# One first transfer for weight half, tokens and gains; conv pieces ahead of the query's; latent transposes five steps behind the key's

## The chip, the cores and the metric

The kernel runs on one core of a Trainium2 chip. The metric is the device time of one execution in microseconds (us): the median of several runs, and beside it the time of the one execution that was profiled. The profile calls the engines PE (TensorE, matmuls), DVE (VectorE), ACT (ScalarE), POOL (GpSimd) and SP (SyncE, which here only issues DMA transfers).

## The reference

Two layers of a streaming-encoder trunk over 256 tokens of width 1024, all in float32. In each layer one combined projection feeds four mixers (latent attention a, pooling b, a spatial gating unit c, a short convolution d), and four gates; then a SwiGLU network follows.

```python
def reference(x, w_in, g_pre_mix, g_cq, g_ckv, w_uq, w_ukv, ...):
    for l in range(DEPTH):
        h = rmsnorm(x, g_pre_mix[l])
        (c_q, c_kv, k_r, p_in, s_u, s_v, cv_b, cv_c, cv_x,
         gate_logits) = split_cols(h @ w_in[l])
        y_a = mla_branch(c_q, c_kv, k_r, g_cq[l], g_ckv[l], w_uq[l], w_ukv[l], cos, sin) @ w_br_a[l]
        y_b = pool_branch(p_in, pool_w[l], pool_scale[l]) @ w_br_b[l]
        y_c = sgu_branch(s_u, s_v, g_sgu_v[l], sgu_w[l], sgu_b[l]) @ w_br_c[l]
        y_d = conv_branch(cv_b, cv_c, cv_x, conv_w[l]) @ w_br_d[l]
        gates = jax.nn.sigmoid(gate_logits).reshape(B, S, N_BRANCH, D)
        merged = (gates[:, :, 0] * y_a + gates[:, :, 1] * y_b
                  + gates[:, :, 2] * y_c + gates[:, :, 3] * y_d)
        x = x + rmsnorm(merged @ w_out[l], g_post_mix[l])
        h = rmsnorm(x, g_pre_ffn[l])
        f = (jax.nn.silu(h @ w_ffn_gate[l]) * (h @ w_ffn_up[l])) @ w_ffn_down[l]
        x = x + rmsnorm(f, g_post_ffn[l])
    return x
```

In mla_branch the latents c_q (256 wide) and c_kv (128) are normalised before the products with w_uq and w_ukv, and the 32 columns of k_r become the rotary part of the key.

## The kernel before, in words

**Weights.** All weights come through in 268 pieces of 128 partitions and up to 1024 columns, in the order of a list (PLAN, from piece_plan). A piece is named by its group: A (latents and rotary key), S (gating unit), P and C (pool and convolution inputs), uq and ukv (the latent attention's second products), g (gates), y (branch products), and so on to the feed-forward. SP issues its transfer into one of four buffers "st"; ACT copies it to a rounded high half (convert, L268), and DVE subtracts this from the piece for the low half (settle, L288). Both halves lie in buffers of the pool "u4", 24 of them. The tokens are split into high and low halves in the same way ("hh" and "hl"), and a product is three matmuls: high by high, low by high, high by low (mac, L318 to L320).

**Order.** One Python program writes the instructions of all engines in order; each engine then runs its own in that order and waits for the others by semaphores. The main line writes matmul units: a unit is one piece for one half of the tokens (h = 0 or 1, 128 tokens each) and mostly six matmuls. After each unit, tick() lets background generators go on by a step, and calls for the next conversions when few converted pieces are ahead. `yield n` in a generator means "go on after n more ticks". Two generators matter here. g_proj belongs to the attention: it normalises the latents (L658 and L659), transposes the rotary keys, copies them into the key's buffers (L665), waits PA ticks, transposes the latents of half 0 and of half 1 (three blocks each, one tick between) and splits them with a gain (split_scaled: ACT L447, DVE L448), then does the query products. g_misc belongs to the other mixers: it transposes z (the convolution's product, two blocks) and p (four blocks) of each half, with copies by ACT at L790, L795 and L796. Both write transposes (L440) through one pool "tp" of two PSUM buffers. The eight PSUM banks are four accumulators "acc", two "mm" and these two.

**Start.** Seven matmuls on zeros warm TensorE up (L387). ACT's queue loads the first 128 rows of the transposed tokens and a table "cst" of 158 columns (rotary tables and all gains); SP's queue loads the first two weight pieces in halves, with the other tokens between. DVE scales the first token block by its gain out of cst (x_hi, L561), ACT converts the first weight halves (L581), and the first matmuls (L909) start.

Of the kernel before, what the change touches and what calls it, by code (L numbers as in the profile page):

```python
# [31 lines left out]
PIECE = 1024  # L32
POOL_W = (2, 4, 8, 16)
PAD = 16
NST = 4
# [3 lines left out]
GF = 5  # L39
GY, MY, AY, AS, MS = 4, 4, 4, 8, 3  # L40
Y1, Y2, Y3, Y4, Y5 = 2, 4, 3, 3, 3
PA, PB = 2, 4
SA, SB = 3, 3
NW = 7
EV = 2
XAT, XD = (8, 9), 8
RN = 1
# [18 lines left out]
SG = {}  # L66
# [4 lines left out]
SGW = _o  # L71


def down_after(b):

    return [b - DLAG] if 0 <= b - DLAG < NB - DLAST else []


def piece_plan():

    plan = []
    for l in range(NL):
        wd = {g: 2 * sum(b - a for a, b in cols) for g, cols in GROUPS}
        if l == 0:
            plan += [((l, g, i), wd[g]) for i in range(4) for g in "AS"]
        else:
            plan += [((l, g, i), wd[g]) for g in "AS" for i in range(4)]
        plan += [((l, "P", i), wd["P"]) for i in range(4)]
        plan += [((l, "uq", i), 1024) for i in range(2)]
        plan += [((l, "ukv", 0), 1024)]  # L90
        plan += [((l, "C", i), wd["C"]) for i in range(4)]
        lag = []
        for br in BRS:
            for n in range(2):
                plan += [((l, "g" + br, n, i), 1024) for i in range(4)] + lag
                lag = [((l, "y" + br, n, i), 1024) for i in range(2 if br == "a" else 1)]
        plan += lag
        for kp in range(2):
# [95 lines left out]


@with_exitstack
def trunk(ctx: ExitStack, tc, x, xT, wall, small, const, qtab, gpost, out):
    nc = tc.nc
    PS = bass.MemoryType.PSUM
    cp = ctx.enter_context(tc.tile_pool(name="cp", bufs=1))  # L200
# [156 lines left out]


    ident = T([P, P], "ident", 1, pool=cp)
    cst = T([P, 96 + NL * SGW], "cst", 1, pool=cp)  # L360
    warm = T([P, 1], "warm", 1, pool=cp)
    ht = [hT_tiles(h) for h in range(2)]
    state["free"] -= 2
# [2 lines left out]
    def xt_load(eng, k0, k1):  # L366
        eng.dma_start(xt[k0 // 4][:, k0 % 4:k0 % 4 + k1 - k0, :], xT[:, k0:k1, :])

    xt_load(nc.scalar, 0, 1)
    nc.scalar.dma_start(cst, const)  # L370
    stage_part(0, 0)
    stage_part(1, 0)
    xt_load(nc.sync, 1, 2)
    stage_part(0, 1)
    stage_part(1, 1)
    state["dma"] = 2
    xt_load(nc.sync, 2, 4)
    stage_to(4)
    xt_load(nc.sync, 4, 6)
    xt_load(nc.sync, 6, 8)  # L380
    wt = tok()
    nc.vector.memset(wt[:, 0:P], 0.0)
    nc.vector.memset(warm, 0.0)
# [170 lines left out]
    sg = gains(0)  # L554
    hT, rstd = [None, None], [None, None]

    def x_hi(k, eng=nc.scalar):
        for h in range(2):
            o, i, g = ht[h][0][:, k, :], xt[k // 4][:, k % 4, h * P:(h + 1) * P], sg["gpm"][:, k:k + 1]
            if eng is nc.vector:  # L560
                nc.vector.tensor_scalar(o, i, g, None, op0=ALU.mult)  # L561
            else:
                nc.scalar.activation(o, i, AF.Identity, scale=g)

    def x_lo(k):
        for h in range(2):
            nc.vector.scalar_tensor_tensor(ht[h][1][:, k, :], xt[k // 4][:, k % 4, h * P:(h + 1) * P],
                                           sg["gpm"][:, k:k + 1], ht[h][0][:, k, :].bitcast(F32),
                                           op0=ALU.mult, op1=ALU.subtract)


    first_w = {i: (U([P, PIECE], F32R), U([P, PIECE], F32R)) for i in range(2)}
    state["free"] -= 4
    src = [staged.pop(i) for i in range(2)]
    for k in range(2):
        x_hi(k, nc.vector if k == 0 else nc.scalar)
        x_lo(k)
        for i in range(2):
            w = PLAN[i][1] // 2
            c = np.s_[:, k * w:k * w + w]  # L580
            nc.scalar.activation(first_w[i][0][c], src[i][c], AF.Copy)  # L581
            nc.vector.tensor_tensor(first_w[i][1][c], src[i][c], first_w[i][0].bitcast(F32)[c], op=ALU.subtract)
    for i in range(2):
        known(i, *first_w[i])
    state["cv"] = 2
    stage_to(5)
    for kp in range(1, 4):
        for k in range(2 * kp, 2 * kp + 2):
            x_hi(k)
            x_lo(k)  # L590
        pump(2)
        settle()
# [601 lines left out]
def build(arrays):  # L1194
    import concourse.bacc as bacc

    nc = bacc.Bacc("TRN2", target_bir_lowering=False, num_devices=1)
    ap = {k: nc.dram_tensor(k, v.shape, F32, kind="ExternalInput").ap() for k, v in arrays.items()}
    out = nc.dram_tensor("out", (SEQ, D), F32, kind="ExternalOutput").ap()
    with tile.TileContext(nc) as tc:  # L1200
        trunk(tc, ap["x"], ap["xT"], ap["wall"], ap["small"], ap["const"], ap["qtab"], ap["gpost"], out)
    return nc


def host_arrays(inputs):
    inp = {k: np.asarray(v) for k, v in inputs.items()}
    wall = np.zeros((len(PLAN), P, PIECE), np.float32)
    for i, (key, w) in enumerate(PLAN):
        wall[i, :, :w] = host_piece(inp, key)
    x = np.ascontiguousarray(inp["x"][0])  # L1210
    const, qtab = host_const(inp)
    return {
        "x": x,
        "xT": np.ascontiguousarray(x.T.reshape(NK, P, SEQ).transpose(1, 0, 2)),
        "wall": wall,
        "small": np.stack([host_small(inp, l) for l in range(NL)]),
        "const": const,
        "qtab": qtab,
        "gpost": np.ascontiguousarray(np.stack([inp["g_post_mix"], inp["g_post_ffn"]], axis=1)),
    }  # L1220
# [9 lines left out]
```

## Time and profile before

| | us |
|---|---|
| median of 3 runs | 802.88 (802.56 to 804.34) |
| the profiled execution | 802.21 |
| its span in the profile | 800.4 |
| mean granted TensorE clock | 0.998 |
| ACT busy, mean of one L268 conversion | 452.6, 1.047 |
| DVE busy, mean of one L288 | 598.3, 1.214 |

The span runs from the first to the last recorded instruction; the rest of the execution's time, 1.81 us, lies around it. Busy times are sums over the span. [...]

### The profile page before, as it was taken

The numbers are of one execution on the slowest core, as the hardware profiler recorded it, in microseconds if no ns is written. First come the engines' busy times: TensorE is split into PE (matmuls) and PEld (weight loads), VectorE is DVE, ScalarE is ACT, GpSimd is POOL, SyncE is SP. The second block draws the span as 40 slices with busy tenths as digits, with TensorE's granted clock in tenths as the row PEclk, the third lists the DMA queues.
The fourth block names the chain that finished last, engine by engine and source line by source line (L and its number), as shares of the span: only waits on it lengthen the run. The fifth ranks groups of instructions, "written<-read, shape, count | busy, mean of one in ns | idle before, by whom it ended". The sixth has DMA issues, their size and how long they took to land.

```text
span 800.4 us, 10903 instructions
## 1 busy us (share of the span) xinstructions
PE 790.8 (99%) x3982; PEld 666.3 (83%) x3982; DVE 598.3 (75%) x1094; ACT 452.6 (57%) x776; POOL 3.9 (0%) x16
## 2 busy tenths in 40 slices
PE   8999999999999999999999999999999999999996
PEld 8888887888888888888888888878888888888885
DVE  6687976758887777778895688764679787777773
ACT  7767655444665555455665675644367555455541
POOL 0000000000000000000000000000000000000000
PEclk9999999999999999999999999999999999999999
DMA  9866444465664565555655545455555555555631
GB/s 317 304 215 212 160 158 158 160 208 164 201 214 136 185 205 185 186 192 176 223 170 197 205 161 182 131 172 197 175 193 184 181 185 186 187 185 185 206 106 52
DMA packets 42245, 148.11 MB, mean 185 GB/s; under 512 B 4688, under 2 KB 5840, under 8 KB 42192
## 3 DMA queue, kind: packets, MB, share of 16 engines
q1 hardware_dynamic: 41328, 145.12, 54.4%
q0 software_dynamic: 576, 2.10, 0.8%
q8 instruction: 31, 0.51, 0.3%
q10 hardware_dynamic: 288, 0.21, 0.1%
q14 instruction: 22, 0.18, 0.1%
HBM read 146.36 MB, written 1.05 MB: 184 GB/s over the span
## 4 chain that ended last, share of the span: by engine, by line
PE 98%; DVE 1%; DMA 0%; ACT 0%; issue 0%; DVEq 0%; SPq 0%; ACTq 0%
PE acc L318 20%; PE acc L320 20%; PE acc L319 20%; PE mm L1097 17%; PE mm L1102 9%; PE tp L440 3%; PE mm L318 2%; PE mm L320 2%; PE mm L319 2%; PE mm L715 1%; PE acc L743 1%; PE acc L909 1%; DMA st<-wall 0%; PE mm L836 0%; PE mm L862 0%; DVE mrg L500 0%
## 5 line engine op out<-in xcount | busy, mean ns | idle before, releaser
L288 DVE TENSOR_TENSOR u<-st,u 128x1024 fp32r<-128x1024 f32 (+1 forms) x268 | 318.6, 1214 | 50.6 <-ACT u L268 50.0
L268 ACT ACTIVATE u<-st 128x1024 fp32r<-128x1024 f32 (+1 forms) x268 | 273.5, 1047 | 17.0 <-DMA st<-wall 16.8
L318 PE MATMUL acc<-u,hh 128*128 128x512 f32 (+1 forms) x424 | 169.1, 399 | 0.0
L320 PE MATMUL acc<-u,hh 128*128 128x512 f32 (+1 forms) x424 | 164.5, 388 | 0.0
L319 PE MATMUL acc<-u,hl 128*128 128x512 f32 (+1 forms) x424 | 164.2, 387 | 0.0
L1097 PE MATMUL mm<-u,u 128*128 128x512 f32 x576 | 144.4, 392 | 0.0
L1097 PEld LDWEIGHTS mm<-u,u 128*128 128x128 f32 x576 | 105.3, 188 | 20.8
L318 PE MATMUL acc<-u,s2k 128*128 128x512 f32 x256 | 101.2, 395 | 0.0
L320 PE MATMUL acc<-u,s2k 128*128 128x512 f32 x256 | 100.6, 393 | 0.0
L319 PE MATMUL acc<-u,s2k 128*128 128x512 f32 x256 | 100.3, 392 | 0.0
L320 PEld LDWEIGHTS acc<-u,hh 128*128 128x128 f32 x424 | 79.6, 188 | 16.2
L318 PEld LDWEIGHTS acc<-u,hh 128*128 128x128 f32 x424 | 79.7, 188 | 14.5 <-issue 0.3
L319 PEld LDWEIGHTS acc<-u,hl 128*128 128x128 f32 x424 | 79.8, 188 | 14.2
L1102 PEld LDWEIGHTS mm<-u,u 128*128 128x128 f32 x576 | 78.6, 190 | 5.6
L1102 PE MATMUL mm<-u,u 128*128 128x256 f32 x576 | 80.3, 282 | 0.0
L1025 ACT ACTIVATE gate<-acc,rhalf 128x512 f32<-128x512 f32 x32 | 22.0, 689 | 65.9 <-PE acc L320 65.7
L320 PEld LDWEIGHTS acc<-u,s2k 128*128 128x128 f32 x256 | 48.1, 188 | 10.1
L318 PEld LDWEIGHTS acc<-u,s2k 128*128 128x128 f32 x256 | 48.2, 188 | 9.3 <-issue 0.3
L319 PEld LDWEIGHTS acc<-u,s2k 128*128 128x128 f32 x256 | 48.1, 188 | 9.1
L1108 DVE TENSOR_TENSOR tok<-mm,tok 128x256 f32<-128x256 f32 x72 | 30.3, 420 | 27.7 <-ACT tok L1107 27.5
L1107 ACT COPY tok<-mm 128x256 f32<-128x256 f32 x72 | 26.6, 370 | 42.6 <-PE mm L1102 39.6
L443 ACT ACTIVATE s2k<-tok 128x256 fp32r<-128x256 f32 (+1 forms) x38 | 16.3, 429 | 53.8 <-DVE tok L1122 53.8
(172 smaller groups left out, 750.1 us busy)
## 6 DMA issues: line engine op xcount, KB each, us to landing
st<-wall SPq DMA_DIRECT2D x261, 512.0 KB, 3.8
st<-wall SPq DMA_DIRECT2D x7, 416.0 KB, 4.0
gpost<-gpost POOLq DMA_DIRECT2D x4, 512.0 KB, 4.7
x<-x SPq DMA_DIRECT2D x2, 512.0 KB, 6.0
small<-small SPq DMA_DIRECT2D x2, 512.0 KB, 4.2
u<-xT SPq DMA_DIRECT2D x3, 256.0 KB, 6.2
st<-wall SPq DMA_DIRECT2D x2, 256.0 KB, 4.3
out<-x SPq DMA_DIRECT2D x2, 256.0 KB, 2.0
```

Of the source, the lines that this page charges most:

```text
L268: nc.scalar.activation(hi[:, :w], st[:, :w], AF.Copy)
L288: nc.vector.tensor_tensor(lo[:, :w], st[:, :w], hi.bitcast(F32)[:, :w], op=ALU.subtract)
L318: nc.tensor.matmul(out_, a[0][aw], w[0][ws], start=start, stop=False)
L319: nc.tensor.matmul(out_, a[1][aw], w[0][ws], start=False, stop=False)
L320: nc.tensor.matmul(out_, a[0][aw], w[1][ws], start=False, stop=stop)
L440: nc.tensor.transpose(dst[:, i * P:(i + 1) * P], s, ident)
L443: nc.scalar.activation(hi, src, AF.Copy)
L1025: nc.scalar.activation(gt[h], pgt[h], AF.Tanh, scale=rhalf[h])
L1097: nc.tensor.matmul(o, pc_[0][:, k * P:(k + 1) * P], hx[k // 2][:, k % 2].rearrange("p s t -> p (s t)"), start=(k == 0), stop=False)
L1102: nc.tensor.matmul(o[:, :SEQ], pc_[1][:, k * P:(k + 1) * P], hx[k // 2][:, k % 2, 0, :], start=False, stop=(k == NK - 1))
L1107: nc.scalar.copy(dst, o[:, SEQ:2 * SEQ])
L1108: nc.vector.tensor_tensor(dst, o[:, 0:SEQ], dst, op=ALU.add)
```

## The change

It has three parts.

1. *The first transfers.* The host writes a new array "head" of two parts. Part 0 is the first half of weight piece 0 (416 columns), the first 128 rows of the transposed tokens (256 columns) and the 8 gain columns of the first norm; part 1 is the other half of the piece, the second 128 rows and the whole table cst. Each comes as one transfer into an "st" buffer. The first block of tokens is scaled with gains read from part 0, the second from part 1, and ACT copies cst out of part 1. ACT issues no transfers any more. Piece 2 is now loaded and converted in two halves as well (split_part), and there is one warm-up matmul more.
2. *The plan.* In each layer the four C pieces come ahead of the two uq pieces and the ukv piece.
3. *PA* goes from 2 to 5: after the rotary keys' transposes, g_proj waits five ticks until it transposes the latents.

```diff
-PA, PB = 2, 4
+PA, PB = 5, 4
...
-NW = 7
+NW = 8
...
         plan += [((l, "P", i), wd["P"]) for i in range(4)]
+        plan += [((l, "C", i), wd["C"]) for i in range(4)]
         plan += [((l, "uq", i), 1024) for i in range(2)]
         plan += [((l, "ukv", 0), 1024)]
-        plan += [((l, "C", i), wd["C"]) for i in range(4)]
...
-    xt_load(nc.scalar, 0, 1)
-    nc.scalar.dma_start(cst, const)
-    stage_part(0, 0)
+    heads = [T([P, PIECE], "st", NST, pool=wp)]
+    nc.sync.dma_start(heads[0][:, 0:HC + HG], head[0, :, 0:HC + HG])
     stage_part(1, 0)
-    xt_load(nc.sync, 1, 2)
-    stage_part(0, 1)
+    heads.append(T([P, PIECE], "st", NST, pool=wp))
+    nc.sync.dma_start(heads[1][:, 0:HC + CW], head[1, :, 0:HC + CW])
     stage_part(1, 1)
-    state["dma"] = 2
     xt_load(nc.sync, 2, 4)
-    stage_to(4)
-    xt_load(nc.sync, 4, 6)
-    xt_load(nc.sync, 6, 8)
+    stage_part(2, 0)
+    stage_part(2, 1)
+    state["dma"] = 3
...
+    def x_in(k, h):
+        if k < 2:
+            return heads[k][:, HA + h * P:HA + h * P + P]
+        return xt[k // 4][:, k % 4, h * P:(h + 1) * P]
+
+    def x_gain(k):
+        if k == 0:
+            return heads[0][:, HC:HC + 1]
+        return heads[1][:, HC + 97:HC + 98] if k == 1 else sg["gpm"][:, k:k + 1]
...
+    def split_part(i, k, src):
+
+        w = PLAN[i][1] // 2
+        c = np.s_[:, k * w:k * w + w]
+        nc.scalar.activation(first_w[i][0][c], src, AF.Copy)
+        nc.vector.tensor_tensor(first_w[i][1][c], src, first_w[i][0].bitcast(F32)[c], op=ALU.subtract)
...
     for k in range(2):
         x_hi(k, nc.vector if k == 0 else nc.scalar)
         x_lo(k)
...
+        split_part(0, k, heads[k][:, 0:HA])
+        split_part(1, k, src[1][:, 512 * k:512 * k + 512])
+    nc.scalar.copy(cst, heads[1][:, HC:HC + CW])
+    stage_to(4)
+    xt_load(nc.sync, 4, 6)
+    for k in range(2):
+        x_hi(2 + k)
+        x_lo(2 + k)
+        split_part(2, k, src[2][:, HA * k:HA * k + HA])
...
     stage_to(5)
-    for kp in range(1, 4):
+    xt_load(nc.sync, 6, 8)
+    pump(1)
+    settle()
+    for kp in range(2, 4):
```

Three places show what moves. Line numbers are each kernel's own: the transposes are L440 before and L445 after, the split L447 and L448 before and L452 and L453 after, the low-half conversions L288 before and L294 after.

The start of SP's queue, before (st is a weight buffer, wall the weights, the "u" from xT the tokens):

```order
L261 DMA st_80<-wall 128x416
L261 DMA st_82<-wall 128x512
L367 DMA u_8_76<-xT 128x256
L261 DMA st_80<-wall 128x416
L261 DMA st_82<-wall 128x512
L367 DMA u_8_76<-xT 128x512
L253 DMA st_88<-wall 128x832
```

The same after; the first and third transfer now carry a weight half, tokens and gains, and the third piece comes in two halves:

```order
L376 DMA st_78<-head 128x680
L267 DMA st_80<-wall 128x512
L379 DMA st_82<-head 128x830
L267 DMA st_80<-wall 128x512
L373 DMA u_8_76<-xT 128x512
L267 DMA st_86<-wall 128x416 x2
L259 DMA st_132<-wall 128x1024
```

TensorE around the latents' transposes of layer 0, before: u_76 holds the latents, tok_545 z of half 0, tok_418 p of half 0; between the first two stand the six matmuls of one unit, between the second and z eighteen.

```order
L440 MATMUL tp_450<-ident_69,kr_458 128x128
L318 MATMUL acc_465<-u_105_481,hh_4_72 128x512
...
L440 MATMUL tp_564<-ident_69,u_76_382 128x128 x3
L318 MATMUL acc_466<-u_105_481,hh_6_74 128x512
...
L440 MATMUL tp_584<-ident_69,u_76_382 128x128 x3
L318 MATMUL acc_605<-u_108_496,hh_4_72 128x512
...
L440 MATMUL tp_641<-ident_69,tok_545 128x128 x2
...
L440 MATMUL tp_668<-ident_69,tok_418 128x128 x4
```

The same after (u_78 the latents, tok_549 z, tok_422 p): eighteen matmuls have come ahead of the first latents' transposes, among them the second gate piece's first ones (u_115, u_116), and z's transposes stand right behind those of half 1, p's one unit later.

```order
L326 MATMUL acc_585<-u_116_541,hh_4_72 128x512
L445 MATMUL tp_608<-ident_69,u_78_386 128x128 x3
L324 MATMUL acc_586<-u_110_500,hh_6_74 128x512
...
L445 MATMUL tp_630<-ident_69,u_78_386 128x128 x3
L445 MATMUL tp_645<-ident_69,tok_549 128x128 x2
L324 MATMUL acc_586<-u_115_540,hh_6_74 128x512
...
L445 MATMUL tp_656<-ident_69,tok_422 128x128 x4
L324 MATMUL acc_585<-u_119_555,hh_4_72 128x512
```

DVE at the same place, before: the key copies, the convolution's product (L937), low halves of weight pieces (L288) and the latents' split of both halves.

```order
L665 COPY u_110_530<-tp_450 64x1024
L665 COPY u_111_531<-tp_450 64x1024
L937 SCALAR_TENSOR_TENSOR tok_545<-acc_465,ry_293,tok_545 128x256
L288 TENSOR_TENSOR u_114_537<-st_421,u_113_536 128x1024
L448 SCALAR_TENSOR_TENSOR s2k_562<-tp_564,cst_70,s2k_560 128x128 x2
L448 SCALAR_TENSOR_TENSOR s2k_563<-tp_564,cst_70,s2k_561 128x128
L288 TENSOR_TENSOR u_118_552<-st_479,u_117_551 128x1024
L937 SCALAR_TENSOR_TENSOR tok_581<-acc_466,ry_293,tok_581 128x256
L448 SCALAR_TENSOR_TENSOR s2k_562<-tp_584,cst_70,s2k_560 128x128 x2
```

After: the order down to the second gate piece's low half (u_116) is the same; the split of half 0 has moved behind another low half and the second product, and one low half (u_132) stands between the two splits.

```order
L693 COPY u_113_535<-tp_454 64x1024
L965 SCALAR_TENSOR_TENSOR tok_549<-acc_469,ry_297,tok_549 128x256
L294 TENSOR_TENSOR u_116_541<-st_425,u_115_540 128x1024
L294 TENSOR_TENSOR u_120_556<-st_483,u_119_555 128x1024
L965 SCALAR_TENSOR_TENSOR tok_571<-acc_470,ry_297,tok_571 128x256
L453 SCALAR_TENSOR_TENSOR s2k_606<-tp_608,cst_70,s2k_604 128x128 x2
L453 SCALAR_TENSOR_TENSOR s2k_607<-tp_608,cst_70,s2k_605 128x128
L294 TENSOR_TENSOR u_132_596<-st_498,u_131_595 128x1024
L453 SCALAR_TENSOR_TENSOR s2k_606<-tp_630,cst_70,s2k_604 128x128 x2
L453 SCALAR_TENSOR_TENSOR s2k_607<-tp_630,cst_70,s2k_605 128x128
```

More of the change, by code (lines that the diff above doesn't have):

```diff
@@ L71 @@
 SGW = _o
+HA = 416
+HC = HA + SEQ
+HG = SG["gpm"][1]
+CW = 96 + NL * SGW
 def down_after(b):
@@ L196, in trunk @@
 @with_exitstack
-def trunk(ctx: ExitStack, tc, x, xT, wall, small, const, qtab, gpost, out):
+def trunk(ctx: ExitStack, tc, x, xT, wall, small, head, qtab, gpost, out):
     nc = tc.nc
@@ L359, in trunk @@
     ident = T([P, P], "ident", 1, pool=cp)
-    cst = T([P, 96 + NL * SGW], "cst", 1, pool=cp)
+    cst = T([P, CW], "cst", 1, pool=cp)
     warm = T([P, 1], "warm", 1, pool=cp)
@@ L367, in xt_load @@
         eng.dma_start(xt[k0 // 4][:, k0 % 4:k0 % 4 + k1 - k0, :], xT[:, k0:k1, :])
-    xt_load(nc.scalar, 0, 1)
-    nc.scalar.dma_start(cst, const)
-    stage_part(0, 0)
+    heads = [T([P, PIECE], "st", NST, pool=wp)]
+    nc.sync.dma_start(heads[0][:, 0:HC + HG], head[0, :, 0:HC + HG])
     stage_part(1, 0)
-    xt_load(nc.sync, 1, 2)
-    stage_part(0, 1)
+    heads.append(T([P, PIECE], "st", NST, pool=wp))
+    nc.sync.dma_start(heads[1][:, 0:HC + CW], head[1, :, 0:HC + CW])
     stage_part(1, 1)
-    state["dma"] = 2
     xt_load(nc.sync, 2, 4)
-    stage_to(4)
-    xt_load(nc.sync, 4, 6)
-    xt_load(nc.sync, 6, 8)
+    stage_part(2, 0)
+    stage_part(2, 1)
+    state["dma"] = 3
+    wt = tok()
     wt = tok()
@@ L555, in trunk @@
     hT, rstd = [None, None], [None, None]
+    def x_in(k, h):
[6 more added lines that the diff above has]
+        return heads[1][:, HC + 97:HC + 98] if k == 1 else sg["gpm"][:, k:k + 1]
     def x_hi(k, eng=nc.scalar):
         for h in range(2):
-            o, i, g = ht[h][0][:, k, :], xt[k // 4][:, k % 4, h * P:(h + 1) * P], sg["gpm"][:, k:k + 1]
+            o, i, g = ht[h][0][:, k, :], x_in(k, h), x_gain(k)
             if eng is nc.vector:
@@ L566, in x_lo @@
         for h in range(2):
[L567 to L574, printed above, removed]
+            nc.vector.scalar_tensor_tensor(ht[h][1][:, k, :], x_in(k, h), x_gain(k),
+                                           ht[h][0][:, k, :].bitcast(F32), op0=ALU.mult, op1=ALU.subtract)
+    def split_part(i, k, src):
[3 more added lines that the diff above has]
+        nc.vector.tensor_tensor(first_w[i][1][c], src, first_w[i][0].bitcast(F32)[c], op=ALU.subtract)
+    first_w = {i: (U([P, PIECE], F32R), U([P, PIECE], F32R)) for i in range(3)}
+    state["free"] -= 6
+    src = [None, staged.pop(1), staged.pop(2)]
     for k in range(2):
@@ L577, in trunk @@
         x_lo(k)
[L578 to L583, printed above, removed]
+        split_part(0, k, heads[k][:, 0:HA])
[7 more added lines that the diff above has]
+        split_part(2, k, src[2][:, HA * k:HA * k + HA])
+    for i in range(3):
         known(i, *first_w[i])
-    state["cv"] = 2
+    state["cv"] = 3
     stage_to(5)
-    for kp in range(1, 4):
+    xt_load(nc.sync, 6, 8)
+    pump(1)
+    settle()
+    for kp in range(2, 4):
         for k in range(2 * kp, 2 * kp + 2):
@@ L1200, in build @@
     with tile.TileContext(nc) as tc:
-        trunk(tc, ap["x"], ap["xT"], ap["wall"], ap["small"], ap["const"], ap["qtab"], ap["gpost"], out)
+        trunk(tc, ap["x"], ap["xT"], ap["wall"], ap["small"], ap["head"], ap["qtab"], ap["gpost"], out)
     return nc
@@ L1211, in host_arrays @@
     const, qtab = host_const(inp)
+    xT = np.ascontiguousarray(x.T.reshape(NK, P, SEQ).transpose(1, 0, 2))
+    head = np.zeros((2, P, HC + CW), np.float32)
+    for k in range(2):
+        head[k, :, 0:HA] = wall[0, :, k * HA:(k + 1) * HA]
+        head[k, :, HA:HC] = xT[:, k, :]
+    head[0, :, HC:HC + HG] = const[:, 96:96 + HG]
+    head[1, :, HC:] = const
     return {
         "x": x,
-        "xT": np.ascontiguousarray(x.T.reshape(NK, P, SEQ).transpose(1, 0, 2)),
+        "xT": xT,
         "wall": wall,
         "small": np.stack([host_small(inp, l) for l in range(NL)]),
-        "const": const,
+        "head": head,
         "qtab": qtab,
```

## The prediction, made before the changed kernel ran

> **What bounds the kernel now.** I began with the page: the span, the busy times and the chain that ended last.
>
> ```profile
> span 800.4 us, 10903 instructions
> ...
> PE 790.8 (99%) x3982; PEld 666.3 (83%) x3982; DVE 598.3 (75%) x1094; ACT 452.6 (57%) x776; POOL 3.9 (0%) x16
> ...
> PE 98%; DVE 1%; DMA 0%; ACT 0%; issue 0%; DVEq 0%; SPq 0%; ACTq 0%
> ```
>
> TensorE is busy for 790.8 of 800.4 us and 98% of the chain is its own. So only two things change the time: matmuls that start earlier at the very beginning and stay earlier, and new holes in TensorE's stream. A hole is not made good later, as there is no idle time on TensorE to fill. The rest of the work was to look at both, in the timeline. First the beginning (columns: start, duration, engine, line, operation, and in brackets the idle time before the row and its releaser).
>
> ```profile
> 1.05 3.36 PE L387 MATMUL mm<-tok 128*128 128x128 f32 x14 [1.05 <-DVE warm L383]
> ...
> 3.50 0.55 ACT L581 ACTIVATE u<-st 128x416 fp32r<-128x416 f32 x1 [0.34 <-DMA st<-wall]
> ...
> 5.24 0.48 DVE L561 TENSOR_SCALAR hh<-u,cst 128x128 fp32r<-128x128 f32 x2 [4.23 <-DMA cst<-const]
> ...
> 5.67 1.03 PE L909 MATMUL acc<-u,hh 128*128 128x416 f32 x2 [1.26 <-ACT u L581]
> ...
> 7.20 1.75 PE L909 MATMUL acc<-u,hh 128*128 128x416 f32 x4
> ...
> 8.74 0.86 PE L909 MATMUL acc<-u,hl 128*128 128x512 f32 x2
> ...
> 10.65 1.02 PE L909 MATMUL acc<-u,hh 128*128 128x416 f32 x4
> ...
> 11.50 0.62 PE L909 MATMUL acc<-u,hl 128*128 128x512 f32 x2
> ```
>
> The warm-up matmuls end at 4.41 and the first real one starts at 5.67. The row names ACT as its releaser, but the conversion of the first weight half was over at 3.50 + 0.55 = 4.05; the last thing to arrive was DVE's scaling at 5.24, which had sat 4.23 us idle for the constant table. That is the wait which the new first transfer attacks. The rows also show half pace: the same four matmuls (two of 416 columns, two of 512) take 8.74 - 7.20 = 1.54 us in the first block and 11.50 - 10.65 = 0.85 in the second.
>
> **Part 1, the start.** In the new order the weight half, the tokens and their gains come in one transfer. Its nearest row is the first weight half of before, converted from 3.50. Scaling (0.48) and conversion (0.55) then end near 4.05, and the warm-up ends later than that: eight instructions are 16 records in place of 14, at 3.36 / 14 = 0.24 each some 0.48 more, so 4.9 by that mean, and 4.6 if the last record's modelled end overstates it. I take 4.75: the first real matmul starts **0.9 us earlier**, and the warm-up hides the rest. If the larger transfer lands late, the gain goes down to nothing.
>
> The half pace may also end earlier. The row at 8.74 is still slow (0.86 for a pair, 0.62 at 11.50), so half pace holds from 5.67 to about 9.2, and costs half of these 3.5 us, 1.7. That is the most to be had; if full pace comes the same time after the first real matmul as before, nothing is. Between 0 and 1.7 I have no nearer row and take the middle, 0.85: **1.75 us** at the start in all, whose size turns out not to matter (part 2).
>
> [...]
>
> Other small changes at the start: the gain table's copy on ACT (158 columns) and the second piece's conversion in two halves are each a part of a microsecond on an engine that is not last there (0.88 us bound: a whole 832-column conversion). I count them at zero while the transfers are the clock of this stretch:
>
> ```profile
> DMA  0004999999999999999999999799789999999999
> GB/s 0 0 0 145 360 360 257 294 346 269 232 338 354 357 425 412 416 395 404 394 407 392 413 360 390 258 239 332 253 335 357 350 350 410 358 395 410 417 395 410
> ```
>
> These are 40 slices of 0 to 22 us. The transfer engines are full from 2.2 us on; only the rate is lower in slices 6 to 11 (257 to 338 GB/s, against about 400 later). At 390 these six would save (390 x 6 - 1736) x 0.55 / 390 = 0.85 us. So the later pieces land between 0 and 0.85 us earlier: their bytes are the same and only their packing differs. I take 0.3.
>
> **Part 2, what the start is worth at 50 us.** The start's gain has to pass a place where TensorE follows DVE closely.
>
> ```profile
> 45.28 1.23 DVE L288 TENSOR_TENSOR u<-st,u 128x1024 fp32r<-128x1024 f32 x1
> ...
> 47.00 2.46 DVE L665 COPY u<-tp 64x1024 f32<-64x1024 f32 x2
> 47.01 0.51 ACT L658 ACTIVATE u<-u,ry 128x256 f32<-128x256 f32 x1 [2.79 <-DVE ry L419]
> ...
> 48.08 0.49 PE L440 MATMUL tp<-ident,u 128*128 128x128 f32 x3
> ...
> 49.84 0.48 DVE L937 SCALAR_TENSOR_TENSOR tok<-acc,ry,tok 128x256 f32<-128x256 f32 x1 [0.38 <-ACT tok L936]
> ...
> 50.24 1.22 DVE L288 TENSOR_TENSOR u<-st,u 128x1024 fp32r<-128x1024 f32 x1
> ...
> 51.98 0.39 PE L320 MATMUL acc<-u,hh 128*128 128x512 f32 x1
> ```
>
> DVE works through two key copies, the conv product and then the low half of the second gate piece, which ends at 51.46. TensorE needs it at 51.98, 0.52 later. The change leaves these rows in this order on DVE. What it moves away is six latent transposes, which used to stand ahead of that matmul: 2 x 0.33 = 0.66 us (three take 0.33, worked out below). So TensorE arrives 0.66 us earlier, plus the start's gain, at data that is ready at 51.46 less what the transfers came earlier. It waits, whether the start has 0.9 or 2.6; and afterwards it still has the six transposes to do. Against before it then stands 0.66 - 0.52 + 0.05 (waking) = 0.2 us late if DVE's chain stays put, and 0.65 early if that chain moves by the full 0.85. With 0.3 it is **-0.1 us**: the start's gain is spent here. ACT's row at 47.01, which waits for the same DVE, shows the other side: with the transposes left where they were, TensorE would have met that scaling, and moving them takes that away.
>
> **Part 3, the transposes five steps behind.** This is in both layers, and here stands the largest term. There are two buffers for transposes. In the new order the latents' three transposes of half 0, one unit, those of half 1 and straight behind them the z transposes of half 0 stand in a row; z must wait until half 0's buffer has been read, by the split (L447 and L448, new L452 and L453). Before, more than two units lay between. The second layer shows the duration of that split, and what TensorE does beside it.
>
> ```profile
> 441.83 0.49 PE L440 MATMUL tp<-ident,u 128*128 128x128 f32 x3
> ...
> 442.39 0.39 PE L319 MATMUL acc<-u,hl 128*128 128x512 f32 x1
> ...
> 442.77 0.35 ACT L447 ACTIVATE s2k<-tp,cst 128x128 fp32r<-128x128 f32 x1
> ...
> 443.49 0.34 DVE L448 SCALAR_TENSOR_TENSOR s2k<-tp,cst,s2k 128x128 fp32r<-128x128 f32 x1
> 443.55 0.49 PE L440 MATMUL tp<-ident,u 128*128 128x128 f32 x3
> ...
> 443.87 0.37 ACT L447 ACTIVATE s2k<-tp,cst 128x128 fp32r<-128x128 f32 x1 [0.74 <-DVE s2k L448]
> ...
> 444.27 0.35 DVE L448 SCALAR_TENSOR_TENSOR s2k<-tp,cst,s2k 128x128 fp32r<-128x128 f32 x1 [0.43 <-ACT s2k L447]
> ...
> 444.65 0.37 ACT L447 ACTIVATE s2k<-tp,cst 128x128 fp32r<-128x128 f32 x1 [0.42 <-DVE s2k L448]
> ...
> 445.05 0.35 DVE L448 SCALAR_TENSOR_TENSOR s2k<-tp,cst,s2k 128x128 fp32r<-128x128 f32 x1 [0.43 <-ACT s2k L447]
> ...
> 445.32 1.22 DVE L288 TENSOR_TENSOR u<-st,u 128x1024 fp32r<-128x1024 f32 x1
> ...
> 446.85 0.34 DVE L448 SCALAR_TENSOR_TENSOR s2k<-tp,cst,s2k 128x128 fp32r<-128x128 f32 x1
> ...
> 448.01 0.38 PE L440 MATMUL tp<-ident,tok 128*128 128x128 f32 x2
> ...
> 451.04 0.60 PE L440 MATMUL tp<-ident,tok 128*128 128x128 f32 x4
> ```
>
> ACT and DVE take turns on the buffer: a pair is 444.65 - 443.87 = 0.78 us, three pairs 2.34. On TensorE 442.39 to 443.55 is five matmuls, 0.232 each; 441.83 to 442.39 is three transposes and one matmul, so three transposes are 0.33 and a unit of six matmuls 1.39.
>
> First wait: the split starts about 0.52 after its transposes do (0.49 and a wake), and frees the buffer at 0.52 + 2.34 = 2.86. TensorE gets to z after 0.33 + 1.39 + 0.33 = 2.05. It waits **0.8 us**.
>
> Second wait: one unit after z come p's four transposes, which need half 1's buffer. On DVE a low-half conversion (1.22, as at 445.32) stands between the two halves' splits, so this buffer is free 1.22 + 0.35 + 2 x 0.78 = 3.13 after the first was. ACT's conversion there is shorter and ends before. TensorE has two transposes (0.22) and a unit (1.39) to do, 1.61. It waits **1.5 us** more. The other two transposes, z and p of half 1, wait for plain copies, with a unit ahead of each, and cost nothing.
>
> So 2.3 us a layer, 4.6 in two. The lower bound is 0 (if the buffers' release is not what holds z and p); the upper is some 3 a layer, if DVE is late with a conversion (1.22) when the first split comes. What waits behind the transposes on TensorE is every later matmul; nothing is moved past them.
>
> **Part 4, other moves.** The four conv pieces come ahead of the query and key-value pieces in both layers. Bytes and conversions are the same and the products that need uq now stand later; zero, with up to 0.2 a layer either way, since TensorE's margin there was between 0.5 and 2 us by the rows around 50.
>
> **Sum.** Profiled execution 802.21 us (span 800.4 and 1.81 around it): 802.21 - 0.1 + 4.6 = 806.7, and a little of the small holes that stand in the stream now will be covered, so **806.5**. The median of before, 802.88, is 0.67 above the profiled execution; I don't add that, because the start, where runs can differ, ends at the same DVE row. Against the median it is +0.45%.
>
> **Rivals.**
> - *The start passes.* DVE's chain at 50 us is early as well, and nothing of the start is lost there: 802.21 - 1.75 + 4.6 = 805.1, and down to 804.2 if all of the half pace goes. For it: the transfers are slower than later in slices 6 to 11. Against: at most 0.85 is to be had there, so half of this has to come from somewhere else, and a faster TensorE doesn't move the row that ends at 51.46.
> - *The buffers don't hold* (the other side). If the pair of ACT and DVE took no more than about 0.5 us instead of 0.78, three would fit into 1.53, and z would not wait; p would follow. With the start's 1.75 it gives 802.21 - 1.75 = 800.5 (799.6 at the most), and with the start spent 802.1. It decides at z's first transpose. Against: each row of the chain waits for the other engine, so the pair is not queueing and has no reason to shrink.
> - *Half the price.* Only one of the two waits shows, or one layer escapes: 2.3 instead of 4.6, 804.2.
> - *The first transfer does nothing.* It lands with the second (conversion at 4.95 now), and real matmuls start at 5.5. At 50 us that is hidden by the same wait: still 806.5.
> - *Worse.* The first split finds DVE busy in both layers, 1.2 each: 808.5.
>
> **How the numbers follow.** Forecast with its two waits in both layers, 0.55 (804.4 to 807.6, the idle first transfer included); the start passes, 0.15 (804.0 to 805.5); half the price, 0.12 (803 to 805); the buffers don't hold, 0.13 (three quarters of it at 799.6 to 801.2, the rest near 802); worse, 0.05. The range goes from 801.8, below half the price and the slower of the free cases, to 807.6. A measurement of this kernel can tell about 0.2% from no change, that is 1.6 us: faster is below 801.3, slower above 804.5. Faster: three quarters of 0.13, 0.10. Same: the rest of it, 0.03, a third of the start's case, 0.05, two thirds of half the price, 0.08, and 0.02 from the forecast's low end, 0.18. Slower: 0.72.
>
> **What would show it.** Right: the first real matmul near 4.75; a TensorE hole just ahead of the second gate piece's low-half matmul near 51.4; in each layer a hole of about 0.8 us before the first z transposes, released by DVE L453, and one of about 1.5 before p's. Wrong: no holes at these transposes, or holes under 0.3; a gate piece whose low half ends well before 51; or a new wait further on, at the query products, which now come later.

## The result, and the profile after

The changed kernel is slower: a median of **811.25 us** over 5 runs (810.52 to 812.34), against 802.80 over 5 runs of the kernel before in the same comparison. The ratio is 1.0106, with a 95% interval of 1.0092 to 1.0119. The forecast was slower by 0.45%, 806.5 with a range of 801.8 to 807.6. So the sign came true, and the size is more than twice the forecast, outside the range. The profiled execution took 810.52 us, 8.3 more than the one of before.

From the page of the changed kernel, the span, the busy times and the chain that ended last:

```profile
span 808.8 us, 10905 instructions
...
PE 794.4 (98%) x3984; PEld 664.7 (82%) x3984; DVE 599.5 (74%) x1095; ACT 452.2 (56%) x778; POOL 3.9 (0%) x16
...
PE 91%; DMA 3%; DVE 3%; ACT 2%; issue 0%; SPq 0%; DVEq 0%; ACTq 0%
```

TensorE's share of the chain has gone from 98% to 91%. But its busy time has grown as well, by 3.6 us, for one more warm-up instruction of 0.43 us at most (two records, 0.213 us from one start to the next). That is the first sign of something that the forecast has no term for.

The start, from the timeline (start, duration, then the instruction, in brackets the idle time ahead of it and its releaser):

```profile
4.37 0.65 PE L937 MATMUL acc<-u,hh 128*128 128x416 f32 x2
...
4.85 0.54 PE L937 MATMUL acc<-u,hl 128*128 128x416 f32 x2
...
7.06 0.69 ACT L578 ACTIVATE hh<-st 128x128 fp32r<-128x128 f32 x2 [1.80 <-DMA st<-head]
...
8.25 0.65 PE L937 MATMUL acc<-u,hh 128*128 128x416 f32 x2 [0.89 <-ACT u L589]
...
10.87 0.35 PE L324 MATMUL acc<-u,hh 128*128 128x416 f32 x1
```

The first real matmul starts at 4.37 in place of 5.67, with no hole in front of it. The matmuls go at full pace almost from there: in the first block 189 to 193 ns from one start to the next with 416 columns and 226 to 236 with 512, but for three of 287 to 297; the slow ones of before are 346 and 427 apart. Then a new hole stands at 8.25: the second block waits for the second head transfer, for which ACT sat idle until 7.06. The first matmul of the third piece, which was at 12.43 before, is at 10.87. The start is 1.56 us ahead.

Further on in the same timeline, the holes of layer 0 and, in the last two rows, of layer 1:

```profile
50.35 0.50 PE L324 MATMUL acc<-u,hh 128*128 128x512 f32 x1 [0.83 <-ACT u L274]
...
51.09 2.35 DVE L294 TENSOR_TENSOR u<-st,u 128x1024 fp32r<-128x1024 f32 x2
...
52.37 0.50 PE L326 MATMUL acc<-u,hh 128*128 128x512 f32 x1 [1.28 <-DVE u L294]
...
53.40 0.49 PE L445 MATMUL tp<-ident,u 128*128 128x128 f32 x3
...
55.13 0.49 PE L445 MATMUL tp<-ident,u 128*128 128x128 f32 x3
...
56.30 0.44 PE L445 MATMUL tp<-ident,tok 128*128 128x128 f32 x2 [0.68 <-DVE s2k L453]
...
59.27 0.66 PE L445 MATMUL tp<-ident,tok 128*128 128x128 f32 x4 [1.16 <-DVE s2k L453]
...
453.97 0.44 PE L445 MATMUL tp<-ident,tok 128*128 128x128 f32 x2 [0.70 <-DVE s2k L453]
...
456.81 0.66 PE L445 MATMUL tp<-ident,tok 128*128 128x128 f32 x4 [1.01 <-ACT tok L818]
```

The second gate piece's low half starts at 51.09 (50.24 before), and TensorE has two holes for that piece. Ahead of z's and p's transposes are the two forecast holes, in both layers. Counted from start to start, against the usual distance of such a pair, the four are 0.85, 1.31, 0.87 and 1.18 us, 4.2 in all, and the two at the gate piece 0.99 and 1.45.

That makes 6.6 of holes less 1.4 of start (by 48 us TensorE is 1.44 ahead of before). Some 3 us of the 8.3 were not holes at all. Compare the two traces matmul by matmul: the distance between one matmul and the next grows evenly between the holes, and only where pool s2k (the split activations) is the operand loaded as weights. Here is such a stretch in the feed-forward part of layer 0, first before, then after; all rows between are the same kind.

```profile
377.14 0.39 PE L318 MATMUL acc<-u,s2k 128*128 128x512 f32 x1
...
383.78 0.39 PE L320 MATMUL acc<-u,s2k 128*128 128x512 f32 x1
```

```profile
381.91 0.40 PE L324 MATMUL acc<-u,s2k 128*128 128x512 f32 x1
...
388.92 0.39 PE L324 MATMUL acc<-u,s2k 128*128 128x512 f32 x1
```

Before, 29 steps take 6.64 us, 229.0 ns each; after, 30 steps take 7.01, 233.7 ns each. (A row's own 0.39 us is longer than the step to the next row, so the rows overlap; what is compared here is the step.) Over the whole kernel the trace has 767 such steps. Taken one by one against the same steps of before they are 4.3 ns longer on average, 3.3 us together. The means that are given from here on leave out the few steps above 330 ns, where something else stands between: 230.7 ns before (763 steps) and 235.3 after (765). The difference of these two means, 4.6 ns or 3.5 us, is the one that the expectations below use; it is a little too large, because two steps of 339 ns before drop out and their partners after, of 320, don't. Of the other forms none that occurs over a hundred times differs by more than 0.9 ns outside of holes. That includes the 120 matmuls that stream s2k and load another operand, while the twelve of the form mm<-u,s2k, which load it, are 4.8 ns further apart as well. Nothing waits in these rows; the matmuls are simply further apart.

What had changed for them is where the pool lies. In the two built programs the pools lie in the order of their first use, and with five steps the latents' split, the first to use s2k, comes after the pools small, rhalf, gpost and mrg. So s2k has gone from 182496 to 199008 in each partition.

### The profile page after: what moved, and what is told of

Same layout as the page of the kernel before. It is cut to its first block, busy times and chain, and to the rows that moved or that the text cites. A ratio compares the mean times of both kernels' runs of the same rounds, so it can differ in the third digit from the quotient of the medians.

```text
span 808.8 us, 10905 instructions
## 1 busy us (share of the span) xinstructions
PE 794.4 (98%) x3984; PEld 664.7 (82%) x3984; DVE 599.5 (74%) x1095; ACT 452.2 (56%) x778; POOL 3.9 (0%) x16
## 4 chain that ended last, share of the span: by engine, by line
PE 91%; DMA 3%; DVE 3%; ACT 2%; issue 0%; SPq 0%; DVEq 0%; ACTq 0%
PE acc L324 19%; PE acc L326 19%; PE acc L325 19%; PE mm L1125 16%; PE mm L1130 8%; PE tp L445 3%; DMA st<-wall 3%; PE mm L326 2%; PE mm L324 2%; PE mm L325 2%; PE mm L743 1%; DVE u L294 1%; PE acc L771 1%; DMA st<-head 1%; ACT u L274 1%; DVE s2k L453 0%
## 5 line engine op out<-in xcount | busy, mean ns | idle before, releaser
L294 DVE TENSOR_TENSOR u<-st,u 128x1024 fp32r<-128x1024 f32 (+1 forms) x267 | 317.7, 1215 | 48.0 <-ACT u L274 48.0
L324 PE MATMUL acc<-u,s2k 128*128 128x512 f32 x256 | 102.8, 401 | 0.0
L325 PE MATMUL acc<-u,s2k 128*128 128x512 f32 x256 | 101.2, 395 | 0.0
L326 PE MATMUL acc<-u,s2k 128*128 128x512 f32 x256 | 101.2, 395 | 0.0
L448 ACT ACTIVATE s2k<-tok 128x256 fp32r<-128x256 f32 (+1 forms) x38 | 16.3, 428 | 53.9 <-DVE tok L1150 53.9
```

Of the source, the lines that this page charges most:

```text
L294: nc.vector.tensor_tensor(lo[:, :w], st[:, :w], hi.bitcast(F32)[:, :w], op=ALU.subtract)
L324: nc.tensor.matmul(out_, a[0][aw], w[0][ws], start=start, stop=False)
L325: nc.tensor.matmul(out_, a[1][aw], w[0][ws], start=False, stop=False)
L326: nc.tensor.matmul(out_, a[0][aw], w[1][ws], start=False, stop=stop)
L448: nc.scalar.activation(hi, src, AF.Copy)
```

## The experiments

The labels ran in four batches, each on one chip beside the kernel before, whose medians there were 802.63 to 802.88, and 803.04 in a single execution beside e13 to e15. Runs with one execution are given without an interval.

**e1: the split buffers' address alone.** One line moves, and no instruction.

```diff
-            yield PA
             ch, cl = [[T([P, 2, SEQ], "s2k", 10, F32R) for _ in range(2)] for _ in range(2)]
+            yield PA
```

> The changed kernel with one line moved: the latents' split buffers (pool s2k) are allocated ahead of the five-step wait, so that this pool lies at its old address again (182496 instead of 199008 in a partition); no instruction moves. In the changed kernel's trace the 765 matmuls acc<-u,s2k of 512 columns start 235.3 ns apart on average, before 230.7; all other forms are within 0.5 ns of before. Theory A (the address of s2k): they go back to about 230.7, and the kernel gains 765 x 4.6 ns = 3.5 us, to about 807.7. Rival B (what runs beside them, or this chip's run): they stay near 235, and the time stays at 811.

808.23 us, ratio to before 1.0068 (1.0049 to 1.0087), 3.0 less than the changed kernel. The mean step went back to 231.0 ns. The view of groups by line and form shows it too (busy time, mean ns of one), first the changed kernel, then e1:

```profile
L324 PE MATMUL acc<-u,s2k 128*128 128x512 f32 x256 | 102.8, 401 | 0.0
L325 PE MATMUL acc<-u,s2k 128*128 128x512 f32 x256 | 101.2, 395 | 0.0
L326 PE MATMUL acc<-u,s2k 128*128 128x512 f32 x256 | 101.2, 395 | 0.0
```

```profile
L324 PE MATMUL acc<-u,s2k 128*128 128x512 f32 x256 | 101.1, 395 | 0.0
L326 PE MATMUL acc<-u,s2k 128*128 128x512 f32 x256 | 100.6, 393 | 0.0
L325 PE MATMUL acc<-u,s2k 128*128 128x512 f32 x256 | 100.4, 392 | 0.0
```

By this run the address is the cause, 235.3 ns at 199008 and 231.0 at 182496; the rival, something beside them or this chip, falls. A matmul's own duration, whose end is modelled, grows by 2 to 6 ns on the three lines; the distance from start to start is the plainer measure.

**e2: z and p later.** `GY, MY, AY, AS, MS = 4, 4, 4, 8, 3` becomes `4, 4, 4, 8, 6`.

> The changed kernel with the z and p transposes' generator started 6 ticks after its spawn instead of 3, in both layers. Theory: the holes ahead of the z and p transposes (0.85 and 1.31 us in layer 0, 0.87 and 1.18 in layer 1, 4.2 in all) are the wait for the two transpose buffers, and go: about 807.0. Rival: they are the split's own lateness and appear in front of whatever comes next (the query products): time within 1 us of 811.

806.83 us, ratio 1.0053 (1.0038 to 1.0068), 4.4 less than the changed kernel. The view of TensorE's waits has none for transposes any more:

```profile
PE acc L326 <- DVE u L294: 1.3, 1, 1.3
PE mm L392 <- DVE warm L388: 1.1, 1, 1.1
PE acc L324 <- ACT u L274: 0.9, 1, 0.9
```

The two buffers were the cause, and nothing took the holes' place.

**e7: both undone, five steps and the start kept.**

```diff
-GY, MY, AY, AS, MS = 4, 4, 4, 8, 3
+GY, MY, AY, AS, MS = 4, 4, 4, 8, 6
...
-            yield PA
             ch, cl = [[T([P, 2, SEQ], "s2k", 10, F32R) for _ in range(2)] for _ in range(2)]
+            yield PA
```

> The changed kernel with both causes taken away and five steps kept: split buffers allocated early (old address) and the z and p transposes' generator started after 6 ticks. If the two prices are separate and add (3.0 to 3.5 and 4.2 to 4.4 measured alone): 811.25 - 3.3 - 4.3 = 803.6. If one hides part of the other: above 805.

803.82 us, ratio 1.0013 (1.0004 to 1.0022). The two prices are separate and add: 7.4 of the 8.45 us. About 1 us is left.

**e10: five steps alone, on the kernel before.** `PA, PB = 2, 4` becomes `5, 4`.

> Five steps alone, on the kernel before: 802.7 + 3.5 (address) + 4.2 (two buffers, two layers) + 0.2 to 0.5 (second gate piece, by the margin of 0.52 against 0.66 of moved transposes) = 810.6 to 811.1, the same as the whole change. DVE's second gate piece stays at 50.2 to 50.5. If the start or the plan adds to the price: below 809.5.

810.97 us, ratio 1.0103 (1.0085 to 1.0121). One number makes the whole loss. The step is 235.3 ns, and these are its holes at the gate piece, at z and at p of layer 0:

```profile
52.18 0.50 PE L320 MATMUL acc<-u,hh 128*128 128x512 f32 x1 [0.20 <-DVE u L288]
...
56.13 0.44 PE L440 MATMUL tp<-ident,tok 128*128 128x128 f32 x2 [0.70 <-DVE s2k L448]
...
58.97 0.66 PE L440 MATMUL tp<-ident,tok 128*128 128x128 f32 x4 [1.01 <-ACT tok L790]
```

Without the new start the gate piece costs 0.20 of idle, not 0.83 and 1.28: there the start's gain is spent. Part of the difference is this execution's own: its TensorE was 0.57 us later than before when the third piece began (13.00 against 12.43). The gate piece's low half on DVE was at 50.92, not within the 50.2 to 50.5 that was expected.

**e4, e9 and e11: the other parts.** e4 is the changed kernel with PA = 2; e9 has the old order of pieces too, which leaves the start alone; e11 is the plan alone on the kernel before.

```diff
         plan += [((l, "P", i), wd["P"]) for i in range(4)]
-        plan += [((l, "C", i), wd["C"]) for i in range(4)]
         plan += [((l, "uq", i), 1024) for i in range(2)]
         plan += [((l, "ukv", 0), 1024)]
+        plan += [((l, "C", i), wd["C"]) for i in range(4)]
```

> The changed kernel with the latents' transposes two steps behind again; the start and the plan stay. Theory: both the holes at the z and p transposes (4.2) and the s2k price (3.5, the pool lies at its old address) go, and the first latents' transposes meet ACT's scaling near 49.3 instead: about 802.8 to 803.5. Rival (the start or the plan has a price of its own in the later parts): above 805.

> The new start alone: the changed kernel with the old order of pieces and two steps. It shows whether the start by itself makes DVE's chain late. Theory (the start moves fewer bytes in the first 20 us, and the later pieces follow): DVE's second gate piece starts at 50.7 to 52 as in all runs with this start so far (50.59 to 52.04), TensorE has a hole of 1.2 to 2 us before the latents' transposes, and the time is 802.0 to 803.0, no gain from matmuls that begin 1.3 us earlier. Rival (the plan or the five steps make the chain late): DVE at 50.3 or earlier, time 801.2 to 801.8.

> The conv pieces ahead of the query pieces alone, on the kernel before: within 0.3 us of 802.7, and DVE's second gate piece at 50.2 to 50.5, as no engine waits for these pieces. Rival: it moves a conversion in front of one that TensorE waits for, a hole of 0.5 or more between 40 and 60 us.

802.75, 802.86 and 802.93 us; the ratios are 1.0002 (0.9992 to 1.0011), 0.9996 (0.9986 to 1.0006) and 1.0002 (0.9993 to 1.0012). Neither part costs or brings anything alone. (e11's low half was at 50.80, again later than expected.) In e4 the whole of the start's gain stands in one row of TensorE's waits:

```profile
PE tp L445 <- ACT u L686: 1.6, 1, 1.6
```

There the latents' transposes meet the scaling, as expected. In e9 the expected hole there was only 0.23 (from start to start); the gain went instead into two waits for low halves, which end at 38.2 and 40.3 us, 0.69 and 0.53. The time is the same. As it reads, what stands in the way is the chain of transfers and conversions, wherever TensorE meets it.

**e3, e5 and e6: why is that chain later with the new start?** e3 puts the heads into the buffer of x and so frees two of the four st buffers; e5 sends the second head as two transfers, and e6 is e5 with PA = 2.

```diff
-    heads = [T([P, PIECE], "st", NST, pool=wp)]
+    xs = T([P, 2, D], "x", 1, pool=cp)
+    heads = [xs[:, k, :] for k in range(2)]
...
-    heads.append(T([P, PIECE], "st", NST, pool=wp))
```

```diff
-    nc.sync.dma_start(heads[1][:, 0:HC + CW], head[1, :, 0:HC + CW])
+    nc.sync.dma_start(heads[1][:, HA:HC + CW], head[1, :, HA:HC + CW])
+    nc.sync.dma_start(heads[1][:, 0:HA], head[1, :, 0:HA])
```

> The changed kernel with the two head transfers going into the buffer of x, which is first written near 14 us, instead of two of the four st buffers. Theory A (the ring): S1's transfer was issued only at 5.30 and A2's at 8.96 because they wait for the heads' buffers; with these free DVE's second gate piece, which started 0.85 us later than before (51.09 against 50.24), is back at about 50.3, and the kernel gains about 0.8, to 810.4. Rival B (one queue with larger packets is slower): it stays at 51, time unchanged.

> The changed kernel with its second head transfer sent as two, tokens and table first, the weight half behind. In the changed kernel ACT sat idle for 1.80 us until 7.06 and DVE for 1.51 until 7.50, waiting for that one transfer of 415 KB; the loss of DMA bytes by 20 us and the 0.85 us at the second gate piece would follow from that. Theory: ACT's second token block starts near 6, DVE's second gate piece comes 0.5 to 1 us earlier than 51.09, and the time goes down by as much, to about 810.4. Rival (the bytes are late whatever the order, since fewer are moved by 20 us): no change at 51, time 811.

> The kernel of the run with two steps behind (802.75), with the second head transfer in two. There the hole ahead of the latents' transposes at 46.53 was 1.77 us, released by ACT's scaling. Theory: DVE and ACT are earlier by 0.5 to 1 us there, the hole shrinks by the same, and the time is 801.8 to 802.3. Rival: unchanged at 802.7.

812.34 (ratio 1.0126, 1.0106 to 1.0145), 811.28 (1.0112, 1.0096 to 1.0127) and 802.71 (1.0000, 0.9990 to 1.0010). Both theories fell. In e5 the second block starts at 5.41 instead of 7.06 and its hole is gone, yet the second gate piece is at 52.04; in e3 the four st buffers are free of the heads and it is at 51.23. e6 had it at 50.59, 0.6 earlier than e4, and its hole ahead of the latents' transposes was 1.40 instead of 1.61, yet its median didn't move.

**e14 and e15: the kernel before, profiled twice more**, for the spread of that chain.

> The kernel before, unchanged, for the spread of its start. If the old start's chain is earlier: DVE's second gate piece at 50.2 to 50.9 again. If it only varies by the run: values above 51 appear.

> As the run ahead of it, once more: DVE's second gate piece at 50.2 to 50.9 if the old start's chain is earlier, above 51 if it only varies by the run.

They took 802.22 and 802.66 us. With the old start the second gate piece's low half begins at 50.24, 50.92 (e10), 50.80 (e11), 50.09 and 50.03, 50.42 on average; with the new one in eleven executions (e12 aside, which moves it) between 50.59 and 52.04, 51.40 on average. So it is later by about 1 us.

Early on, one reason can be seen. The sixth weight piece shows it, on ACT, before and after:

```profile
14.52 1.06 ACT L268 ACTIVATE u<-st 128x1024 fp32r<-128x1024 f32 x1 [0.38 <-DMA st<-wall]
```

```profile
15.92 1.06 ACT L274 ACTIVATE u<-st 128x1024 fp32r<-128x1024 f32 x1 [1.76 <-DMA st<-wall]
```

This conversion starts at 14.0 to 14.8 in the five executions with the old start and at 15.2 to 16.7 in the eleven with the new one that keep the heads in st buffers. In e3, which frees those buffers, it starts at 14.74. So there the heads' buffers do hold the pieces up, as far as one execution of e3 shows it. But that doesn't settle what happens at 50 us. e3 falls behind again between 21 and 25 us. And in the changed kernel's own trace DVE had caught up by the low half at 33.59 (33.72 before), and lost 0.33 and 0.51 at the next two pieces, for which ACT waited for transfers.

The new start also moves fewer bytes early. The windows of before and after (the last two columns are the share of DMA time and GB/s):

```profile
0.00:5.00 5.00, 3.36 (x14) 3.06 (x14) 0.17 (x2) 2.09 (x4) 0.69 (x6) 1.00 0.64 197
5.00:10.00 5.00, 4.33 (x13) 3.85 (x14) 4.76 (x14) 4.07 (x10) 0.00 (x0) 1.00 1.00 357
10.00:15.00 5.00, 5.00 (x27) 4.63 (x26) 4.18 (x8) 4.06 (x8) 0.00 (x0) 1.00 0.98 359
15.00:20.00 5.00, 5.00 (x26) 4.47 (x25) 4.55 (x8) 4.34 (x10) 0.00 (x0) 1.00 1.00 355
```

```profile
0.00:5.00 5.00, 3.94 (x19) 3.93 (x20) 1.41 (x7) 2.41 (x4) 0.69 (x6) 1.00 0.63 179
5.00:10.00 5.00, 4.11 (x20) 3.12 (x19) 3.38 (x8) 3.17 (x9) 0.00 (x0) 1.00 0.99 331
10.00:15.00 5.00, 5.00 (x25) 4.30 (x24) 4.44 (x11) 4.15 (x10) 0.00 (x0) 1.00 0.92 317
15.00:20.00 5.00, 5.00 (x26) 4.50 (x25) 3.43 (x7) 3.88 (x7) 0.00 (x0) 1.00 0.95 331
```

In 20 us that is (197 + 357 + 359 + 355) x 5 GB/s x us = 6.34 MB before and 5.79 MB after, 1.5 us of transfer at the 357 GB/s that before moved from 5 to 10 us. These two executions lie far apart, though: over all of them it is 5.95 to 6.34 MB with the old start and 5.76 to 6.12 with the new one, and e15, with the earliest chain of all, moved the 5.95. By 40 us the kernel before has moved 12.41 MB and the changed one 12.43. e3 brings the rate back to 358 and 363 GB/s between 5 and 15 us, and the chain is still late. So the bytes are not shown to be the cause, and why the chain is late at 50 us stays open.

**e8 and e13: which addresses are slow?** Both allocate the split's first buffers in the main line, e8 behind rhalf (address 186720), e13 ahead of it (186592).

```diff
+        lat = [[T([P, 2, SEQ], "s2k", 10, F32R) for _ in range(2)] for _ in range(2)]
         rhalf = [T([P, 1], "rhalf", 4) for _ in range(2)]
...
-            ch, cl = [[T([P, 2, SEQ], "s2k", 10, F32R) for _ in range(2)] for _ in range(2)]
+            ch, cl = lat
```

> The changed kernel with the split buffers allocated between rhalf and gpost, so that pool s2k lies at 186720 (a multiple of 2048 plus 352, as 199008 is), inside the region that it had before (182496 to 202976, a multiple of 2048 plus 224). Theory A (the offset within 2048 decides): acc<-u,s2k stays near 235.3 ns. Theory B (the region decides): near 231.

> The changed kernel with pool s2k at 186592, allocated between small and rhalf: a place of its own, a multiple of 2048 plus 224 as before the change. Theory (the offset within 2048 decides): acc<-u,s2k at 230.7 to 231 ns, the time near 808. Rival (any place but the old one is slow): 235.3, 811.

e8 took 811.03 us with steps of 235.3 ns, e13 807.7 with 231.0. The two places are 128 bytes apart, and overlap the old region; what they share with the slow and the fast case is the offset in 2048, 352 and 224. Of the other pools only rhalf lies elsewhere in one than in the other. (A smaller modulus that tells the two apart, 256 or 512, would do as well; that wasn't tried. Nor was the streamed operand's pool moved, so whether the offset counts by itself or against the other operand's address isn't known.) The instruction's own duration in the feed-forward end of layer 0, e8 and then e13 (minimum, median and maximum in ns):

```profile
L324 PE MATMUL acc<-u,s2k x28: 393/398/479, 382.4 to 401.8; 128*128 128x512 f32 x28
```

```profile
L324 PE MATMUL acc<-u,s2k x29: 388/388/478, 381.1 to 401.3; 128*128 128x512 f32 x29
```

**e12: a version that lets the start pass.** On top of e7, the latents' scaling (ACT) and the key copies (DVE), which stand ahead of the second gate piece on both engines and are not needed for it, go two ticks behind the key's transposes.

```diff
+            transposes(t, [krs[h].rearrange("p n d -> p (n d)") for h in range(2)])
+            ch, cl = [[T([P, 2, SEQ], "s2k", 10, F32R) for _ in range(2)] for _ in range(2)]
+            yield PC
             for h in range(2):
                 nc.scalar.activation(a_sb[h][:, 0:256], a_sb[h][:, 0:256], AF.Identity, scale=r4[:, 2 * h:2 * h + 1])
...
-            transposes(t, [krs[h].rearrange("p n d -> p (n d)") for h in range(2)])
             kT[:] = [keep([P, 4, SEQ]) for _ in range(2)]
...
-            yield PA
-            ch, cl = [[T([P, 2, SEQ], "s2k", 10, F32R) for _ in range(2)] for _ in range(2)]
+            yield PA - PC
```

> The changed kernel with both prices taken away as in the run of 803.82, and g_proj's latent scaling (ACT) and key copies (DVE) moved two ticks behind the key transposes, so that the second gate piece's conversion stands ahead of them on both engines. There the holes at 49.5 (1.07, released by ACT's conversion) and 51.2 (1.45, by DVE's) made up for the start's gain. Theory: these two go, 2.5 us: 801.2 to 801.6, below before. Rival (the same engines are late with the next thing): a hole of like size at the next gate piece or at the latents' transposes, 803 or more.

**801.14 us**, ratio 0.9978 (0.9969 to 0.9988): 1.7 below the kernel before, 10.1 below the changed one. From DVE's and TensorE's timeline, and TensorE's waits:

```profile
48.29 1.22 DVE L294 TENSOR_TENSOR u<-st,u 128x1024 fp32r<-128x1024 f32 x1
49.54 2.46 DVE L695 COPY u<-tp 64x1024 f32<-64x1024 f32 x2
...
56.66 0.50 PE L326 MATMUL acc<-u,hh 128*128 128x512 f32 x1 [0.42 <-DVE u L294]
```

```profile
PE mm L392 <- DVE warm L388: 1.1, 1, 1.1
PE acc L326 <- DVE u L294: 0.4, 1, 0.4
```

The gate piece's low half is at 48.29, ahead of the copies, and its two holes are gone. One of 0.42 stands at a later gate piece. For the first time part of the start's gain is kept to the end: TensorE is 1.34 us ahead of the kernel before at 47.9 us, 0.93 ahead at 147, and 0.94 at 793. These moves were not run with the old start, so how much of the 1.7 us is the start's is not shown.

## Why the prediction was right in sign and wrong in size

**The start (part 1): mechanism right, sizes off both ways.** The first matmul began 1.30 us earlier, not 0.9: the warm-up's 16 records took 3.50 us, not 3.84, and the first real matmul is put over the last of them. Half pace was over at once in the profiled execution (191 ns from the second matmul to the third, 346 before); over the runs with the new start, between none and seven of the first twelve matmuls were slow. The new hole at the second block (0.89) wasn't foreseen. With it the start came to 1.56 where 1.75 was forecast, so that the near agreement is luck. As argued, its size didn't matter to the time: the start alone took 802.86 (e9).

**The gate piece (part 2): mechanism right, term mis-sized.** The start's gain is spent there; e10 against the changed kernel, and e12, show it. But the term was -0.1 and came out near +1: ahead by 1.4, then held for 0.99 + 1.45. The step that failed here is "the later pieces land between 0 and 0.85 us earlier: their bytes are the same and only their packing differs". They landed later, the sixth by 1.4 us, and DVE's chain came 0.85 us late in place of 0.3 early. Put into the prediction's own sum, 0.66 - 0.52 + 0.05 + 0.85 gives 1.04, as measured; for the 0.05 of waking, 0.06 lie between the low half's end at 52.31 and the matmul at 52.37. The prediction looked at the packing alone, and not at the two st buffers that the heads hold, which by e3 is what delays the early pieces (the sixth starts at 14.74 there, at 15.92 in the changed kernel); why the chain is late at 50 us is open.

**The two buffers (part 3): right in layer 0, the second wait of layer 1 by another path.** Forecast 0.8 and 1.5 us a layer; measured 0.85 and 1.31, 0.87 and 1.18, so 4.2 for 4.6. The chain of three pairs was there as read, and e2 shows that the buffers are the cause, which the rivals "the buffers don't hold" and "half the price" denied. But in layer 1 the releaser of p's transposes is ACT's copy of z (L818), not the split of half 1 (in e10 this is so in layer 0). There the program gave p the buffer that z had just used. The copy that empties it stands behind half 1's split in ACT's order:

```profile
456.13 0.37 ACT L452 ACTIVATE s2k<-tp,cst 128x128 fp32r<-128x128 f32 x1 [0.42 <-DVE s2k L453]
456.39 0.36 ACT L818 COPY tok<-tp 128x256 f32<-128x256 f32 x1
```

The low-half conversion delays both paths, so the two sizes are close; that the second layer's fits is in part luck.

**"So only two things change the time": this is the step that failed most.** The two things were matmuls that start earlier and new holes in TensorE's stream. Every matmul that doesn't move was taken to cost what it had cost. The five steps moved an allocation too, and with it 767 matmuls became 4.3 ns slower: 3.3 us by the traces, 3.0 by e1's medians. That is most of the 4.0 us by which the profiled execution (810.52) lies above the forecast. The prediction's own sum, 806.7, with 3.3 for the address, 1.1 more at the gate piece and 0.4 less at the buffers gives 810.7, where 810.52 was measured. No row of the trace of before shows what another address costs, but the addresses of a built program can be compared before it runs, and weren't. Part 4 itself, zero for the conv pieces, was right (e11).

Two slips in the working changed nothing: the six slices of the transfer rate run from 232 to 346 GB/s, not from 257 to 338 (their sum is right), and the rival "worse" comes to 808.9, not 808.5.

**Sum.** By medians, the address 3.0 (e1), the buffers 4.4 (e2) and the rest 1.0 to 1.2 (e7 against before) give 8.4 to 8.6, where 8.45 was measured.

## What to carry to other kernels

When a change moves the first use of a buffer, compare the addresses of all pools in the two built programs; if one that feeds the matrix engine has moved, time that alone (it was 3.0 us here, by e1). A chain through a few buffers could be priced here by the rows of its steps, before it was met (4.2 us for 4.6). And the earlier start was worth nothing until the next engine that TensorE follows closely had been made earlier as well: a gain came only once the work that nobody there needed was moved out of its way.

## What the runs showed of the hardware

- In the fifteen programs timed here the distance between the matmuls that load s2k as weights went with the address of that pool: at an offset of 224 in 2048 bytes (182496 and 186592), 230.6 to 231.0 ns in nine programs; at 352 (199008 and 186720), 235.1 to 235.3 ns in six (changed kernel, e2, e3, e5, e8, e10). In e1, e8 and e13 only the place of the allocation differs from the changed kernel. The waits show nothing of it, and no other offset was run. What makes it so is not shown.
- Before, the first matmuls stand 346 ns apart with 416 columns and 427 with 512 up to 9.2 us, and about 190 and 230 after. Executions with the same start differ in where this half pace ends, from the first real matmul (changed kernel) to about 2.6 us behind it (e9). The clock column shows 1.00 there. In e10 it shows 0.78 of full clock between 5 and 10 us and 0.88 between 10 and 15; in that trace the first matmuls ran at full pace, and half pace came from 7.8 to 11.2 us.
- A share of DMA time near 1.00 is no fixed rate: in the changed kernel 331 GB/s stand beside 0.99 (5 to 10 us) and 415 beside 1.02 (20 to 25 us).
